# RWKV-7 block on one core: the intra-chunk product of w over 128 rows, and the router's 16 columns streamed eight times

## The chip, the cores and the metric

The kernel runs on one core of one Trainium2 chip. The metric is the device time of one execution in microseconds (us). Three runs of the kernel before took 3162.34, 3146.18 and 3159.18 us, median 3159.18 us.

## What is computed

The reference is one block of a diffusion backbone, over 2048 latent tokens with a prefix of 256 context tokens, width 1024, all in float32. Cut to what bears on the change:

```python
# RWKV-7 time mixing, 8 heads of 64, forward and backward over the tokens
def step(s, inp):
    r_t, w_t, k_t, v_t, a_t, b_t = inp
    sa = einsum('bhvk,bhk->bhv', s, a_t)
    s = s * w_t + sa[..., None] * b_t + v_t[..., None] * k_t
    return s, einsum('bhvk,bhk->bhv', s, r_t)
...
x = x + g1 * (concat([a_x, b_x]) @ w_out)     # time mixing and a short gated convolution
hx = modulate(rmsnorm(x, norm2_g), sh2, sc2)
aff = softmax(hx @ router_w)                  # 16 experts: 16 columns
vals, idx = top_k(swapaxes(aff, 1, 2), 256)   # each expert takes its 256 best tokens
x = x + g2 * scatter_add(silu(xs @ w_gate) * (xs @ w_up) @ w_down * vals)
return rmsnorm(x, final_g)
```

## The kernel before

The program goes through four stages. `proj_phase` (to about 620 us) makes the projections. `wkv_phase` (about 620 to 1860 us) runs the recurrence and fills TensorE's time with other work: the convolution's projections (`conv_gen`, line 262), the convolution's share of the output projection (`conv_out_gen`, line 985), and, from step 20 on, `out_gen`: group norm, output projection, norm and router. `topk` (about 1900 to 1960 us) picks the tokens, and `moe_phase` runs the 16 experts.

The recurrence is cut into chunks of 64 tokens: 4 of context and 32 of latent tokens, so 36 steps s, each for two directions d, forward and backward. For a step and a direction:

- `front` (line 782) multiplies the scaled keys with the scaled queries for all 8 heads and masks the products into `g`, which holds for each head a 128 x 128 block. `solve` (lines 818, 820, on VectorE) and `merge` (lines 839 and 843 on TensorE, copy at line 844 on ScalarE) replace the upper left 64 x 64 part of each block, rows 0 to 63, with the inverse of a triangular matrix.
- `tokmaj` turns the keys to token order (line 798) and allots `uv`, a tile of 128 x 8 x 64 with three buffers: rows 64 to 127 get the values V by a transfer on SyncE's queue (line 803), rows 0 to 63 are written much later with the solved u (line 870).
- `chain` holds the dependent part. `wy` = state times `ar` (line 857: 4 matmuls of 128 rows, 128 columns); then, for each of 8 heads, the intra-chunk part of w is added from rows 64 to 127 of `g` and of `uv` (line 860); ScalarE copies it to `w` (line 863); line 869 applies the inverse, ScalarE copies the result into rows 0 to 63 of `uv` (line 870); line 877 makes the update of the state, VectorE adds it and writes the state `Sb` (lines 883, 886), GpSimd writes the copy `sc` (line 888); line 895 makes the output y.

```python
for h in range(H):
    nc.tensor.matmul(wy[0:64, h], g[64:128, d, hx(h), 0:64], uv[64:128, h], start=False, stop=True, ...)
w = ws[d]
nc.scalar.copy(w[0:64], wy[0:64])
```

The router (`route`, line 1111) is called for each of 16 tiles of 128 tokens: 8 matmuls, each with a 128 x 128 block of the normed tokens as weights and 16 columns of the router's matrix `rt` streamed through. `back` reads the 16 columns of logits from PSUM.

Every float32 matmul is two instructions in the trace; those on the rounded halves ("H" and "L" tiles) are one.

The order of instructions on each engine is not the order of the Python text. The program is traced, and a planner with a simulated time line orders the instructions of each engine by their priority and the time at which it thinks they can start; each engine then runs its own list in order. GpSimd's list in this stage holds part of the scaling of keys and queries (line 766), the copies `sc` (line 888), parts of the convolution and of the second modulation (line 201), and the group norm's gating (lines 1061, 1062). SyncE's list holds the loads and stores, the transfer of V among them. A new `uv` tile can be written only when the tile three before it has been read for the last time, and the planner keeps track of which rows of a tile each instruction touches.

Of the kernel before, what the change touches and what calls it, by code (L numbers as in the profile page):

```python
# [20 lines left out]
KT = 8  # L21
# [9 lines left out]
NE = 16  # L31
# [11 lines left out]
def _dap(t, off, ap):  # L43
    a = t[tuple(slice(None) for _ in t.shape)] if not isinstance(t, bass.AP) else t
    return bass.AP(tensor=a.tensor, offset=a.offset + off, ap=ap)


def two(t, w, j, off=0, n=None):

    lo = NCL // 2 - 1 - j  # L50
    return [_dap(t, c * C * w + off, [[w, C], [1, n or w]]) for c in (lo, lo + 2 * j + 1)]


def two_in(nc, x, rows):

    for q, r in enumerate(rows):
        nc.sync.dma_start(x[64 * q:64 * q + 64], r)
# [636 lines left out]
def wkv_phase(ctx_, tc, k, I, S, fill):  # L694
    nc = tc.nc
    with ExitStack() as ctx:
# [30 lines left out]
        hx = lambda h: h % 2 * HP + h // 2  # L727
        pre = {}

        def tok0(isctx, c):  # L730
            return c * C if isctx else TC + c * C
# [61 lines left out]
        def tokmaj(s, d):  # L793
            isctx, c = order[d][s]
            bk = slots[s, d][2]
            pt = psum.tile([128, HP, 128], F32, name="pbt", tag="pu", bufs=2)
            for p in range(HP):
                nc.tensor.transpose(pt[:, p, :], bk[:, p], k.ident)
            bt = sb.tile([128, HP, 128], F32, name="bt", bufs=2)
            nc.scalar.copy(bt, pt)  # L800
            slots[s, d][2] = bt
            uv = sb.tile([128, H, C], F32, name="uv", bufs=3)
            nc.sync.dma_start(uv[64:128], _dap(S["V"], tok0(isctx, c) * 512, [[512, 64], [64, H], [1, 64]]))
            slots[s, d][3] = uv

# [40 lines left out]
        def chain(s):  # L846
            st_ = []
            if s >= TURN:
                k.y[s] = k.bp.tile([128, H, C], F32, name="oy", tag="ev", bufs=5)
                two_in(nc, k.y[s].rearrange("p h c -> p (h c)"), two(S["Y"], 512, s - TURN))  # L850
            for d in range(2):
                isctx, c = order[d][s]
                ar, g, bt, uv, pc = slots.pop((s, d))
                so = sn = Sb[d]
                wy = psum.tile([128, H, C], F32, name=f"wy{d}")
                for p in range(HP):
                    nc.tensor.matmul(wy[:, 2 * p:2 * p + 2], ar[:, p], so[:, p], start=p == 0, stop=False,
                                     skip_group_check=True)
                for h in range(H):
                    nc.tensor.matmul(wy[0:64, h], g[64:128, d, hx(h), 0:64], uv[64:128, h], start=False, stop=True,  # L860
                                     skip_group_check=True)
                w = ws[d]
                nc.scalar.copy(w[0:64], wy[0:64])
                st_.append((isctx, c, ar, g, bt, uv, pc, so, sn, wy, w))
            for d in range(2):
                isctx, c, ar, g, bt, uv, pc, so, sn, wy, w = st_[d]
                pu = psum.tile([64, H, C], F32, name="pu", bufs=2)
                for h in range(H):
                    nc.tensor.matmul(pu[:, h], g[:, d, hx(h), 0:64], w[:, h], start=True, stop=True)
                nc.scalar.copy(uv[0:64], pu)  # L870
            for d in range(2):
                isctx, c, ar, g, bt, uv, pc, so, sn, wy, w = st_[d]
                if s < NS - 1:
                    sp = psum.tile([128, HP, C], F32, name="ps", tag="pu", bufs=2)
                    for h in range(H):
                        r = slice(64 * (h % 2), 64 * (h % 2) + 64)
                        nc.tensor.matmul(sp[r, h // 2], bt[:, h // 2, r], uv[:, h], start=True, stop=True)
                    f = pc if d == 0 else slots[s + 1, d][4]
                    sc = sb.tile([128, HP, C], F32, name="sc", bufs=4)
                    if s == 0:  # L880
                        nc.vector.tensor_copy(sc, sp)
                    else:
                        nc.vector.tensor_tensor(sc, sp, Sc[d], op=OP.add)
                    for par in range(2):
                        r = slice(64 * par, 64 * par + 64)
                        nc.vector.tensor_tensor(sn[r, :, 64 * par:64 * par + 64], sc[r],
                                                f[r].unsqueeze(2).to_broadcast([64, HP, C]), op=OP.mult)
                    nc.gpsimd.tensor_tensor(sc, sc, f.unsqueeze(2).to_broadcast([128, HP, C]), op=OP.mult)
                    Sc[d] = sc
            for d in range(2):  # L890
                isctx, c, ar, g, bt, uv, pc, so, sn, wy, w = st_[d]
                if isctx:
                    continue
                for h in range(H):
                    nc.tensor.matmul(wy[64:128, h], g[:, d, hx(h), 64:128], uv[:, h], start=False, stop=True,
                                     skip_group_check=True)
                if s < TURN:
                    nc.scalar.copy(uv[64:128], wy[64:128])
                    nc.sync.dma_start(S["Y"][c * C:c * C + C, :], uv[64:128].rearrange("p h t -> p (h t)"))
                else:  # L900
                    half = slice(64 - 64 * d, 128 - 64 * d)
                    nc.vector.tensor_tensor(k.y[s][half], wy[64:128], k.y[s][half], op=OP.add)
# [8 lines left out]
        def ready(s):  # L911
            if s < NS:
                merge(s)
                for d in range(2):
                    tokmaj(s, d)
# [17 lines left out]
        for s in range(NS):  # L933
            chain(s)
            ready(s + 1)
            if s % 2:
                scale((s + 5) // 2)
            begin(s + AHEAD)
            fill(75 // 20 + 1 if s < TURN else 100, s >= TURN)
            if s == TURN:  # L940
                fill(0, True)
# [71 lines left out]
def out_gen(tc, k, I, S):  # L1013

    nc = tc.nc
    bp = k.bp
    wo = load_wo(tc, k, I, S, 0)
    rt = k.cp.tile([128, KT, NE], F32, name="rt")
# [87 lines left out]
        return z  # L1106

    def route(pl, z, n):
        for q in range(4):
            kt = 4 * n + q  # L1110
            nc.tensor.matmul(pl[:, :NE], z[:, q], rt[:, kt], start=kt == 0, stop=kt == KT - 1)

    def spots(j):
        return (slice(0, 64), NCL // 2 - 1 - j), (slice(64, 128), j)
# [10 lines left out]
    def back(j, x, lt=None):  # L1125
        ss = sm("oss", 1)
        square(x, ss)
        r2 = root(ss)
        zs = [flat(j, x, n) for n in range(2)]
        pl = k.bps.tile([128, 512], F32, name="pj")  # L1130
        for n in range(2):
            route(pl, zs[n], n)
        if lt is not None:
            nc.vector.scalar_tensor_tensor(lt, pl[:, :NE], r2, bb, op0=OP.mult, op1=OP.add)
        for half, i in spots(j) if lt is None else ():
            nc.vector.scalar_tensor_tensor(k.lg[half, i % 4, i // 4], pl[half, :NE], r2[half], bb[half], op0=OP.mult,
                                           op1=OP.add)
        if lt is not None:
            return r2
        spill(j, x, r2, "act")  # L1140
# [18 lines left out]
    pl = k.wps.tile([128, 512], F32, name="pl", tag="pu", bufs=2)  # L1159
    for n in halves(LAST, x, y):  # L1160
        square(x[:, 512 * n:512 * n + 512], sums[:, n:n + 1])
        route(pl, flat(LAST, x, n), n)
# [495 lines left out]
```

## Time and profile before

| | |
|---|---|
| median of 3 runs | 3159.18 us (3146.18 to 3162.34) |
| the profiled execution | 3142.96 us |
| its span, first to last instruction | 3141.1 us |
| mean granted TensorE clock over the span | 0.93 |
| TensorE busy (matmuls) | 2881.8 us, 92% |
| VectorE / ScalarE / GpSimd busy | 68% / 44% / 21% |

[...] A row with "x16" merges sixteen instructions in a row, and its time is from the start of the first to the end of the last.

### The profile page before, as it was taken

Reading aid. Unit: us, or ns where it says so; the run is one execution under the profiler, and the core shown is the slowest. Engines: PE = TensorE matmul, PEld = TensorE weight load, DVE = VectorE, ACT = ScalarE, POOL = GpSimd, SP = SyncE. Lnnn points to the kernel's source line nnn. Section 1 sums busy time; section 2 is a strip of 40 time slices with the busy share of each in tenths; the row PEclk is TensorE's granted clock in tenths of the full one; section 3 lists DMA queues with packets and bytes.
Section 4 is the critical chain, followed back from the end, with each engine's and each line's share of the span. In section 5 each row is a group of like instructions: output and inputs, shape, how many; then the busy total and the mean of one; then the engine's idle time right before and its main releaser. Section 6 shows DMA issues by size and latency. Waiting matters only on the chain. (4 is left out here: it accounts for less than half of the span.)

```text
span 3141.1 us, 62585 instructions
## 1 busy us (share of the span) xinstructions
PE 2881.8 (92%) x24367; PEld 2612.9 (83%) x24367; DVE 2141.5 (68%) x4611; ACT 1385.0 (44%) x2279; POOL 667.4 (21%) x893
## 2 busy tenths in 40 slices
PE   6988989889999999999999994999999999999997
PEld 4877978878888888778888873998999899999886
DVE  7688687766666666667767646666666666666776
ACT  6556645423344443224445443444444444444453
POOL 0243242533333322112222121000000000000011
PEclk8989999977999999998788986999999999999998
DMA  6466555666666655766665551666666666666886
GB/s 248 144 201 193 178 175 170 201 170 152 154 169 165 173 141 162 204 176 169 164 151 143 124 165 47 201 219 205 188 204 204 195 197 208 207 203 206 267 285 228
DMA packets 408745, 577.43 MB, mean 184 GB/s; under 512 B 175864, under 2 KB 257912, under 8 KB 407424
## 3 DMA queue, kind: packets, MB, share of 16 engines
q1 hardware_dynamic: 397504, 533.58, 56.4%
q0 software_dynamic: 10656, 38.80, 5.3%
q8 instruction: 191, 3.13, 0.4%
q10 hardware_dynamic: 288, 1.05, 0.1%
q14 instruction: 106, 0.87, 0.1%
HBM read 444.73 MB, written 128.59 MB: 183 GB/s over the span
## 5 line engine op out<-in xcount | busy, mean ns | idle before, releaser
L129 ACT CAST wH<-wr 128x1024 fp32r<-128x1024 f32 (+1 forms) x592 | 528.9, 897 | 844.7 <-PE pg L1429 408.8
L134 DVE TENSOR_TENSOR wL<-wr,wH 128x1024 fp32r<-128x1024 f32 (+1 forms) x586 | 627.6, 1076 | 353.5 <-ACT wH L129 347.6
L1429 PE MATMUL pg<-xH,wH 128*128 128x256 f32 x2048 | 585.4, 286 | 15.8 <-ACT s L1433 15.8
L1429 PE MATMUL pg<-xL,wH 128*128 128x256 f32 x2048 | 576.2, 282 | 0.0
L1429 PE MATMUL pg<-xH,wL 128*128 128x256 f32 x2048 | 575.7, 281 | 0.0
L262 PE MATMUL pj<-hH,wH 128*128 128x256 f32 x1600 | 478.0, 299 | 25.5 <-ACT cu L671 7.4
L262 PE MATMUL pj<-hH,wL 128*128 128x256 f32 x1600 | 469.4, 294 | 23.6 <-DVE wL L134 22.6
L262 PE MATMUL pj<-hL,wH 128*128 128x256 f32 x1600 | 468.1, 293 | 1.4 <-DVE hL L134 1.1
L1429 PEld LDWEIGHTS pg<-xH,wH 128*128 128x128 f32 x2048 | 389.5, 190 | 17.9 <-ACT s L1433 16.5
L1429 PEld LDWEIGHTS pg<-xL,wH 128*128 128x128 f32 x2048 | 389.3, 190 | 1.5
L1429 PEld LDWEIGHTS pg<-xH,wL 128*128 128x128 f32 x2048 | 389.5, 190 | 0.0
L262 PEld LDWEIGHTS pj<-hH,wH 128*128 128x128 f32 x1600 | 318.4, 199 | 37.6 <-DVE cu L674 8.4
L262 PEld LDWEIGHTS pj<-hH,wL 128*128 128x128 f32 x1600 | 316.6, 198 | 30.9 <-DVE wL L134 28.9
L262 PEld LDWEIGHTS pj<-hL,wH 128*128 128x128 f32 x1600 | 318.5, 199 | 5.6 <-DVE hL L134 2.0
L1488 POOL DMA_INDIRECT ACC<-o,it x30 | 50.8, 1694 | 954.4 <-DVE o L1474 800.7
L1446 PE MATMUL pd<-wH,hL 128*128 128x512 f32 x512 | 201.9, 394 | 0.0
L1446 PE MATMUL pd<-wL,hH 128*128 128x512 f32 x512 | 201.9, 394 | 0.0
L1446 PE MATMUL pd<-wH,hH 128*128 128x512 f32 x512 | 199.9, 395 | 0.0
L818 DVE TENSOR_TENSOR x<-X,x 128x120 f32<-128x120 f32 (+12 forms) x540 | 157.8, 296 | 57.7 <-DMA X<-TI 46.0
L820 DVE TENSOR_TENSOR X<-X,x 128x120 f32<-128x120 f32 (+12 forms) x540 | 163.0, 305 | 12.3
L782 PE MATMUL pg<-ar,bk 64*128 64x128 f32 x1152 | 141.0, 323 | 17.1 <-DVE g L784 7.5
L782 PEld LDWEIGHTS pg<-ar,bk 64*128 64x128 f32 x1152 | 114.4, 215 | 33.7 <-issue 13.5
(428 smaller groups left out, 5456.9 us busy)
## 6 DMA issues: line engine op xcount, KB each, us to landing
wr<-in_w_gate_dram SPq DMA_DIRECT2D x128, 512.0 KB, 4.2
wr<-in_w_up_dram SPq DMA_DIRECT2D x128, 512.0 KB, 4.8
wr<-in_w_down_dram SPq DMA_DIRECT2D x128, 512.0 KB, 3.3
wr<-in_w_in_dram SPq DMA_DIRECT2D x208, 256.0 KB, 3.2
bk<-KBD SPq DMA_DIRECT2D x36, 512.0 KB, 5.6
ar<-NR SPq DMA_DIRECT2D x36, 512.0 KB, 5.9
adaw<-in_ada_b_dram SPq DMA_DIRECT2D x32, 512.0 KB, 3.7
inc<-C SPq DMA_DIRECT2D x36, 256.0 KB, 3.1
```

The source lines that it names most:

```text
L129: nc.scalar.copy(H_, src)
L134: (leng or nc.vector).tensor_tensor(L_, src, H_.bitcast(F32), op=OP.subtract)
L262: nc.tensor.matmul(ps, wa[:, kw, :], ha[:, kt, :], start=m == 0, stop=m == 3 * KT - 1)
L782: nc.tensor.matmul(pg[:, p], bk[rows, p], ar[rows, p], start=True, stop=True)
L818: nc.vector.tensor_tensor(tv, X[:, 0:r, t:t + 1].to_broadcast([128, r, m]), x[:, t:t + 1, t + 1:].to_broadcast([128, r, m]), op=OP.mult)
L820: nc.vector.tensor_tensor(X[:, 0:r, t + 1:], X[:, 0:r, t + 1:], tv, op=OP.add)
L1429: nc.tensor.matmul(ps, a[:, ws], b[:, kt], start=i == 0, stop=i == 23)
L1446: nc.tensor.matmul(po[2 * m + n], a[:, f, ms], b[:, ns], start=f == 0 and q == 0, stop=f == FB - 1 and q == 2)
L1488: nc.gpsimd.indirect_dma_start(out=S["ACC"], out_offset=bass.IndirectOffsetOnAxis(ap=ids[m][:, :1], axis=0), in_=o, in_offset=None, comput ...
```

## The change

A memset on GpSimd zeroes rows 0 to 63 of each new `uv` tile. The intra-chunk matmul of w then runs over all 128 rows of `g` and `uv`: the upper 64 rows add products with zeros. The router's 16 columns are read eight times over (a stride of zero), so that each router matmul streams 128 columns and writes 128 columns of PSUM, of which the first 16 are used as before.

```diff
@@ tokmaj
             uv = sb.tile([128, H, C], F32, name="uv", bufs=3)
+            nc.gpsimd.memset(uv[0:64], 0.0)
             nc.sync.dma_start(uv[64:128], _dap(S["V"], tok0(isctx, c) * 512, [[512, 64], [64, H], [1, 64]]))
@@ chain
                 for h in range(H):
-                    nc.tensor.matmul(wy[0:64, h], g[64:128, d, hx(h), 0:64], uv[64:128, h], start=False, stop=True,
+                    nc.tensor.matmul(wy[0:64, h], g[:, d, hx(h), 0:64], uv[:, h], start=False, stop=True,
                                      skip_group_check=True)
@@ route
         for q in range(4):
             kt = 4 * n + q
-            nc.tensor.matmul(pl[:, :NE], z[:, q], rt[:, kt], start=kt == 0, stop=kt == KT - 1)
+            nc.tensor.matmul(pl[:, :128].rearrange("p (a e) -> p a e", e=NE), z[:, q],
+                             rt[:, kt].unsqueeze(1).to_broadcast([128, 128 // NE, NE]), start=kt == 0, stop=kt == KT - 1)
```

## Rows read from the trace of the kernel before

**Rows 1.** The page: busy time of the engines, and granted clock in 40 slices.
```profile
PE 2881.8 (92%) x24367; PEld 2612.9 (83%) x24367; DVE 2141.5 (68%) x4611; ACT 1385.0 (44%) x2279; POOL 667.4 (21%) x893
...
PEclk8989999977999999998788986999999999999998
```

**Rows 2.** Busy time by stretch; after the engines granted clock, DMA share, GB/s.
```profile
620.00:800.00 180.00, 156.73 (x1367) 143.46 (x1367) 118.01 (x279) 58.85 (x97) 64.26 (x96) 0.74 0.68 172
800.00:1440.00 640.00, 602.76 (x6357) 538.13 (x6355) 423.91 (x963) 231.85 (x394) 171.23 (x236) 0.97 0.62 167
1440.00:1895.00 455.00, 435.11 (x4346) 374.94 (x4344) 296.98 (x1014) 212.43 (x420) 108.72 (x158) 0.86 0.61 152
```

**Rows 3.** By stretch, router (L1111) alone: PE, PEld, granted clock, DMA share, GB/s.
```profile
1464.70:1495.20 30.50, 1.86 (x16) 1.86 (x16) 1.00 0.49 127
1495.40:1512.30 16.90, 0.00 (x0) 0.00 (x0) 0.50 0.80 210
...
1529.60:1536.20 6.60, 0.33 (x2) 0.22 (x2) 0.50 0.66 161
...
1539.90:1543.00 3.10, 0.00 (x0) 0.00 (x0) 0.50 0.47 157
...
1563.80:1570.30 6.50, 0.39 (x2) 0.29 (x2) 0.50 0.64 155
...
1594.50:1611.20 16.70, 0.00 (x0) 0.00 (x0) 0.50 0.37 89
...
1632.00:1635.10 3.10, 0.00 (x0) 0.00 (x0) 0.50 1.19 193
...
1656.00:1669.00 13.00, 3.59 (x16) 3.48 (x16) 0.50 0.60 132
...
1697.00:1703.00 6.00, 3.60 (x16) 3.49 (x16) 0.50 0.98 175
...
1816.30:1819.40 3.10, 0.00 (x0) 0.00 (x0) 0.50 0.02 5
...
1878.00:1880.90 2.90, 0.00 (x0) 0.00 (x0) 0.50 0.99 353
```

**Rows 4.** The same for the intra-chunk matmuls of w (L860) alone.
```profile
741.10:778.40 37.30, 3.93 (x32) 3.56 (x32) 0.50 0.64 158
1444.20:1464.50 20.30, 3.93 (x32) 3.55 (x32) 0.50 0.79 209
```

**Rows 5.** The time line of TensorE just before the fall at 1495.3 us.
```profile
1492.96 1.86 PE L1111 MATMUL pj<-rt,oxt 128*128 128x16 f32 x16
```

**Rows 6.** The time line, 1440 to 1480 us: runs of weight loads, one per matmul.
```profile
1441.41 1.64 PEld L1027 LDWEIGHTS pj<-rb,ones 128*128 128x128 f32 x14
...
1446.63 1.77 PEld L860 LDWEIGHTS wy<-uv,g 64*64 64x64 f32 x16 [0.22 <-issue]
...
1457.61 1.78 PEld L869 LDWEIGHTS pu<-w,g 128*64 128x64 f32 x16 [0.22 <-issue]
...
1468.03 0.97 PEld L857 LDWEIGHTS wy<-Sb,ar 128*128 128x128 f32 x8
...
1477.44 0.54 PEld L860 LDWEIGHTS wy<-uv,g 64*64 64x64 f32 x8
```

**Rows 7.** GpSimd's memset of line 716: count, shortest, median, longest in ns.
```profile
L716 POOL MEMSET w<- x2: 520/521/522, 618.9 to 619.3; 64x512 f32 x2
```

**Rows 8.** The time line at 1758 us: V is asked for, and w starts.
```profile
1758.40 0.45 SPq L803 DMA_DIRECT2D uv<-V  x1
...
1762.98 1.14 PE L860 MATMUL wy<-uv,g 64*64 64x64 f32 x16 [1.99 <-DMA uv<-V]
```

**Rows 9.** The time line at 1526 us: w starts ahead of merge's last copy.
```profile
1526.29 1.14 PE L860 MATMUL wy<-uv,g 64*64 64x64 f32 x16
...
1538.22 0.57 ACT L844 COPY g<-pm 32x512 f32<-32x512 f32 x1 [1.14 <-PE pm L843]
```

**Rows 10.** GpSimd's waits, 630 to 1900 us: total us, times, longest.
```profile
POOL sc L888 <- DVE Sb L886: 262.2, 64, 24.0
```

## The prediction

> **What bounds the kernel now.** I read the page first: TensorE is busy 92% of the span, no other engine passes 68%, and the granted clock, slice by slice, is below 0.9 in few places [rows 1]. [...] I then cut the span by stage [rows 2]. The recurrence has two weak stretches: 620 to 800 us, with a mean clock of 0.74, and 1440 to 1895 us, with 0.86. Between them, with the convolution's 256-column matmuls as filler, it is 0.97. [...]
>
> The third view asks what TensorE did before each fall. In 1440 to 1895 us I count 15 stretches at 0.50. Nine of them follow straight on the router's matmuls [rows 3]. The first: 16 of them end at 1494.8 us [rows 5], and the clock is 0.50 from 1495.3 to 1512.4 us. The same happens at 1529, 1564, 1594 and 1632 us, and four more times from 1816 to 1881 us, of which the first and the last are shown. These nine are 16.9 + 6.6 + 6.5 + 16.7 + 3.1 us, and 15.4 us for the last four: 65.2 us. A tenth, 3.1 us at 1540 us, follows on 16 matmuls of line 860, the intra-chunk part of w. Inside three more low stretches the two edited kinds stand too: 32 of line 860 in 741 to 778 us and 32 in 1444 to 1464 us [rows 4], 16 router matmuls in each of 1656 to 1669 and 1697 to 1703 us [rows 3]; four stretches, 37.3 + 20.3 + 13.0 + 6.0 = 76.6 us.
>
> What the edited kinds share is that TensorE is occupied by them and does little: the router streams 16 columns for every 128 x 128 load of weights, line 860 uses half the rows. The change fills the empty columns and rows.
>
> **Router.** 128 matmuls, 256 instructions. Fourteen instructions of the same form, 128 rows with 16 columns (line 1027), take 1.64 us at the full clock, 0.117 each; eight with 128 columns (line 857) take 0.97, 0.121 each [rows 6]. The weight load sets the distance in both. So widening costs 0.004 us each by these rows, 256 x 0.004 = 1.0 us, and I take 1. The bounds are 0 and, if the streaming did not hide, the whole of a 128-column instruction again, 31 us.
>
> **w over 128 rows.** Sixteen of line 860 take 1.77 us at the low clock, sixteen of line 869, which already are 128 rows by 64 columns, 1.78 [rows 6]. 1152 instructions at nothing each: 0 us, bounds 0 and 1152 x 0.001 = 1 us.
>
> **The memset.** 72 of them, the size of line 716: 0.521 us each [rows 7], 37.5 us more on GpSimd, which is busy 109 of 455 us in the late stretch [rows 2]. It needs the same buffer to come free as the transfer of V, and w waits for both. The shortest of the 72 distances from the issue of V to w's first matmul is 4.6 us [rows 8], with w waiting for V at its end. The memset fits nine times. I take 0, with ends of 0 and 37.5 us: the cover is the transfer of V and, after it, GpSimd's idle time. What it can run into is GpSimd's own list: behind the memset stand the scaling of keys and queries and `sc`, ahead of it may stand an instruction that waits.
>
> **The added dependence on merge.** w now reads rows 0 to 63 of `g`, so it waits for merge's copy (line 844). In 28 of 36 steps that copy ends before w begins. In eight it doesn't, the shown one by 12.5 us [rows 9]; in the first step w ran 78 us ahead for nothing. In these w moves behind the copy, but line 869 has to wait for the copy anyway, so what is added to the chain is w itself and its copy: 16 x 0.068 = 1.1 us [rows 6] and about 0.6 us like the copy shown, 1.7 us, 7 times: 12 us of the recurrence. TensorE has other work queued (it idles 20 of 455 us), so I take 3 us, with ends of 0 and 12. Next in line behind w's copy is line 869, which is late by as much.
>
> **The clock.** [...] Of the 76.6 us in the four other stretches the fall itself stays, as other narrow work stands before it, and I let the clock come back halfway through: 38 us, a gain of 19. Sum 53 us, with ends of 0 and (68.3 + 76.6) / 2 = 72. Not all of it arrives: work that runs faster meets waits (in rows 2 VectorE is busy 297 of 455 us), and new falls can appear where there was none, since every instruction moves. I keep eight tenths: 42 us.
>
> Sum: 42 - 1 - 0 - 3 = 38 us off. Against the profiled execution, 3142.96 us, that is 3105 us. That execution was 16.2 us faster than the median of the three runs; from the median, 3159.18, it is 3121 us, which I forecast.
>
> **Rival: no difference.** The clock may follow only the time for which TensorE is occupied, not how much of it. Then filling columns and rows, at the same distance from matmul to matmul, changes nothing, and the time is the median plus the costs, 3159 + 4 = 3163 us. Against it: in 1440 to 1895 us TensorE is occupied 96% of the time, more than the 94% of the stretch before, and has the lower clock [rows 2]. [...] A second road to the same result: the planner gets other costs (128 columns instead of 16, a memset, a new dependence), reorders the stage, and as many falls come up elsewhere. Chance of both together 0.20.
>
> **Rival: slower.** The memset sits on GpSimd's list behind the `sc` of the step before, which waits for the state (64 waits, 262 us, the longest 24 us [rows 10]). The state is also what line 857 starts from, and from there to w lie only its 0.97 us. Where the memset starts after `sc`, it can end after line 857 and w waits; each such wait idles TensorE, and in the stretch where it idles most (157 of 180 us busy) the clock is lowest [rows 2], so the gain goes too. It decides as soon as the memset ends over 0.97 us after the state. The price is at most the memset for each of 72 tiles, 37.5 us: 3159 + 37 = 3197 us. Against it: the buffer comes free 4.6 us or more before w, mostly while `sc` of the step before is not yet due, and a planner that places by readiness puts the memset early. Chance 0.10.
>
> **Numbers.** The forecast, with its gain anywhere from 16 to 75 us, has 0.70. A difference of 0.5%, 16 us, is about what a measurement of this kernel can tell from none (the three runs span 16 us). The low end is the whole of the clock's 72 us and a little for falls that I did not count: 3082 us. The high end takes in the no-difference rival with all of the merge's 12 us, 3171 us; it leaves out most of the slower rival. Of the forecast's 0.70 some 0.02 falls short of 16 us, and of the no-difference rival some 0.04 still gains over 16: faster 0.72, same 0.18, slower 0.10.
>
> **What would show it.** In the profile after: the granted clock in the stretch from step 21 to the top-k at 0.93 or more, and no fall straight behind the router; the router's 16 instructions still within 1.9 us, line 860's sixteen within 1.1 us at the full clock; line 860 now shown as 128 rows; 72 memsets of about 0.52 us and no long wait of line 860 for them; TensorE's total busy time down by some 40 us, nearly all between 1440 and 1895 us, and the stages before 620 us and after the top-k as long as they were. The prediction is wrong if the router's widened matmuls are still followed by falls, if the number of low stretches stays at about fifteen, if waits for GpSimd stand among TensorE's largest, or if the time saved lies in a stage that the edits don't touch.

## The result, and the profile after

The change takes 3106.82 us (median of 4 runs, 3096.77 to 3115.09), the kernel before beside it 3152.68 us: a ratio of 0.9866, 95% interval 0.9828 to 0.9904, so 1.3%, or some 42 us by the ratio and 46 us by the medians. The forecast was a gain of 38 us.

The profiled execution after took 3115.09 us (span 3113.2 us, granted clock 0.945). The page, and busy time by stretch with the columns of [rows 2]; PE is TensorE's matmuls, PEld its weight loads, and the granted clock is a share of full speed:

```profile
PE 2823.5 (91%) x24367; PEld 2567.4 (82%) x24367; DVE 2151.2 (69%) x4611; ACT 1379.1 (44%) x2275; POOL 701.1 (23%) x965
...
PEclk8989999979999999999999996999999999999998
```
```profile
620.00:800.00 180.00, 146.08 (x1436) 134.66 (x1434) 123.53 (x291) 62.83 (x104) 73.53 (x113) 0.85 0.68 178
800.00:1440.00 640.00, 596.89 (x6270) 535.25 (x6266) 424.32 (x942) 229.62 (x389) 187.59 (x268) 0.96 0.61 166
1440.00:1895.00 455.00, 399.25 (x4457) 345.68 (x4456) 329.08 (x1158) 220.10 (x457) 130.84 (x199) 0.93 0.62 156
```

TensorE runs the same 24367 matmuls and is busy 58 us less; the span of this execution is only 28 us shorter, so TensorE also idles 30 us more. The stretch from 1440 to 1895 us has a clock of 0.93 instead of 0.86 [rows 2], although it now also holds the beginning of the top-k, where TensorE is nearly idle.

Where the time went is read from the starts of two kinds of matmul. Lines of one source line each: count, shortest, median, longest ns, first and last start. First the top-k's first matmul before, then the router and the same top-k matmul after:

```profile
L1258 PE MATMUL pa<-ident,lg x16: 311/311/365, 1900.2 to 1901.5; 64*64 64x64 f32 x16
```
```profile
L1113 PE MATMUL pj<-rt,oxt x240: 275/275/582, 1498.4 to 1862.4; 128*128 128x128 f32 x120
...
L1261 PE MATMUL pa<-ident,lg x16: 311/311/365, 1868.6 to 1869.9; 64*64 64x64 f32 x16
```

From the first router call to the top-k it was 1900.2 - 1493.0 = 407.2 us [rows 5] and is 370.2 us: 37 us less. From there to the end it is 1240.9 and 1244.6 us, and the projections ahead took about 9 us longer in this execution; neither is touched by the change. From the recurrence's first matmul (line 782) to the first router call it is 862.9 and 859.5 us, 3 us less; that stretch returns further down.

The same stage after, with the columns of [rows 3] and of the router alone; the stretches are cut where the clock changes:

```profile
1474.80:1478.00 3.20, 0.00 (x0) 0.00 (x0) 0.50 1.03 228
1478.20:1505.30 27.10, 2.05 (x16) 1.86 (x16) 1.00 0.54 161
...
1529.40:1536.00 6.60, 3.78 (x16) 3.49 (x16) 0.50 0.87 198
...
1573.90:1676.00 102.10, 5.95 (x48) 5.60 (x48) 1.00 0.66 163
...
1751.30:1853.50 102.20, 10.75 (x80) 9.54 (x80) 1.00 0.54 150
1853.70:1856.90 3.20, 0.00 (x0) 0.00 (x0) 0.50 1.01 394
```

Nine falls are left where there were fifteen, and they hold some 37 us instead of 123. None comes straight behind the router. One stretch of 102 us holds 48 router instructions at full clock, another 80. What stands before a fall now is, for example, this, on the time line just ahead of the fall at 1474.7 us:

```profile
1469.23 1.15 PE L861 MATMUL wy<-uv,g 128*64 128x64 f32 x16
1472.80 1.12 PE L861 MATMUL wy<-uv,g 128*64 128x64 f32 x16 [2.42 <-DMA uv<-V]
1473.84 0.81 PE L840 MATMUL pm<-tz,g 32*32 32x32 f32 x20
```

The widened w stands there with a wait for V, in which TensorE idled 2.42 us. A pause of this kind stands ahead of all nine. The rows below take the 4 us ahead of a fall, with the columns of [rows 2]: the figure behind the comma is how long TensorE was busy in them. First come two of the falls behind the router before the change, then three of the nine after it, namely the one shown, the one with the most idle time and the one with the least:

```profile
1491.30:1495.30 4.00, 4.00 (x60) 3.75 (x57) 3.91 (x20) 1.16 (x2) 0.71 (x1) 1.00 0.64 148
1590.30:1594.30 4.00, 4.00 (x41) 3.72 (x42) 3.88 (x25) 1.46 (x4) 0.00 (x0) 1.00 0.50 114
```
```profile
1470.70:1474.70 4.00, 1.90 (x37) 1.82 (x38) 2.36 (x15) 0.87 (x2) 1.74 (x2) 1.00 0.68 187
1501.40:1505.40 4.00, 0.07 (x2) 0.10 (x2) 4.00 (x9) 3.41 (x10) 2.48 (x3) 1.00 0.82 280
1535.50:1539.50 4.00, 3.12 (x67) 2.65 (x66) 3.61 (x15) 1.16 (x2) 0.00 (x0) 0.92 1.08 203
```

Before the change, ahead of nine of the fifteen falls, TensorE had idled less than 0.3 of those 4 us. These nine held some 85 of the 123 us, and eight of them had matmuls of 16 columns within the 4 us. Ahead of the other six it had idled 1.2 to 3.4 us. After the change it had idled 0.9 to 3.9 us ahead of every one of the nine. So there were two kinds of falls, those without a pause and those behind a pause, and only the second kind is left. Which part of the change does what is the question of the experiments.

### The profile page after: what moved, and what is told of

Same layout as the page of the kernel before. It is cut to its first block, busy times and chain, and to the rows that moved or that the text cites. A ratio compares the mean times of both kernels' runs of the same rounds, so it can differ in the third digit from the quotient of the medians.

```text
span 3113.2 us, 62779 instructions
## 1 busy us (share of the span) xinstructions
PE 2823.5 (91%) x24367; PEld 2567.4 (82%) x24367; DVE 2151.2 (69%) x4611; ACT 1379.1 (44%) x2275; POOL 701.1 (23%) x965
## 5 line engine op out<-in xcount | busy, mean ns | idle before, releaser
L819 DVE TENSOR_TENSOR x<-X,x 128x120 f32<-128x120 f32 (+9 forms) x540 | 163.0, 305 | 65.7 <-DMA X<-TI 53.3
L821 DVE TENSOR_TENSOR X<-X,x 128x120 f32<-128x120 f32 (+9 forms) x540 | 168.1, 314 | 12.0
L782 PE MATMUL pg<-ar,bk 64*128 64x128 f32 x1152 | 125.0, 312 | 31.8 <-POOL em L749 8.1
L782 PEld LDWEIGHTS pg<-ar,bk 64*128 64x128 f32 x1152 | 103.8, 208 | 47.5 <-POOL ar L766 11.5
```

What stands on the lines that cost most here:

```text
L782: nc.tensor.matmul(pg[:, p], bk[rows, p], ar[rows, p], start=True, stop=True)
L819: nc.vector.tensor_tensor(tv, X[:, 0:r, t:t + 1].to_broadcast([128, r, m]), x[:, t:t + 1, t + 1:].to_broadcast([128, r, m]), op=OP.mult)
L821: nc.vector.tensor_tensor(X[:, 0:r, t + 1:], X[:, 0:r, t + 1:], tv, op=OP.add)
```

## The experiments

Theory: the clock follows how much of the array TensorE fills while it is occupied, and both parts of the change fill it. Rivals: the gain is only another order of instructions; or it is one part's alone; or the memset costs time. Every run lists its mean granted clock c, and the low-clock time below (the time at a granted clock of 0.50) is 2 (1 - c) x span, averaged over a kernel's executions. That takes the clock to be either 1.00 or 0.50: of 10470 pieces of 0.3 us in the profiled execution before, 8966 are at 1.00, 1406 at 0.50 and 98 between them. As an estimate, half of the low-clock time is what a higher clock can save: sixteen of the router take 1.86 us at 1.00 and 3.48 us at 0.50 [rows 3]. The low-clock time is that of the whole program; of the 440 us before, some 125 lie in the router's stage. Each ratio is to the runs of the kernel before that were taken beside that kernel (their medians lie between 3145.53 and 3152.68 us), so two kernels are better compared by their ratios than by their medians.

| kernel | median us | ratio to before (95%) | mean clock | low-clock us |
|---|---|---|---|---|
| before (the 29 runs beside the router alone) | 3147.95 | | 0.930 | 440 |
| whole change, first | 3106.82 | 0.9866 (0.9828 to 0.9904) | 0.947 | 328 |
| whole change, again | 3100.66 | 0.9867 (0.9844 to 0.9890) | 0.948 | 324 |
| router at 128 alone | 3101.55 | 0.9842 (0.9815 to 0.9868) | 0.944 | 349 |
| w over 128 rows, with the memset | 3136.15 | 0.9973 (0.9950 to 0.9996) | 0.938 | 391 |
| memset alone | 3139.47 | 0.9961 (0.9940 to 0.9982) | 0.931 | 434 |
| router at 32 | 3139.40 | 0.9978 (0.9950 to 1.0005) | 0.936 | 403 |
| router at 64 | 3110.69 | 0.9889 (0.9866 to 0.9912) | 0.940 | 373 |
| router at 256 | 3145.26 | 1.0000 (0.9978 to 1.0021) | 0.942 | 363 |
| router and its bias at 128 | 3108.23 | 0.9878 (0.9852 to 0.9904) | 0.944 | 350 |
| memset, w's first head over 128 rows | 3149.30 | 1.0006 (0.9980 to 1.0031) | 0.933 | 421 |
| whole, merge in its own tile | 3119.73 | 0.9912 (0.9877 to 0.9947) | 0.946 | 339 |
| router at 128, merge in its own tile | 3102.04 | 0.9853 (0.9816 to 0.9890) | 0.948 | 322 |
| whole, four uv buffers | 3126.65 | 0.9927 (0.9900 to 0.9954) | 0.945 | 343 |

### One part at a time

**The router alone.** Line 860 as before, and no memset.

> Only the router is widened to 128 columns; w keeps 64 rows and there is no memset. Theory (the clock follows how much of the array TensorE fills while it is occupied): the nine low stretches behind the router, 65 us, go, the fall behind w stays; gain 65 / 2 x 0.8 = 26 us, so about 3127 us against a median before of 3153; low-clock time in the stage from the first router call to the top-k from 123 us down to about 60. Rival 1 (the gain is only another order of instructions): falls still come straight behind the router, and the gain can be anything, as large in the kernel with 32 columns. Rival 2 (the gain comes from w alone): 3153 us, within 8.

3101.55 us: the whole gain, 46 us by the medians, where 26 were expected. The low-clock time falls by 440 - 349 = 91 us, and half of that is 45 us. Nothing else is needed to explain it.

**w alone.**

```diff
+            nc.gpsimd.memset(uv[0:64], 0.0)
-  nc.tensor.matmul(wy[0:64, h], g[64:128, d, hx(h), 0:64], uv[64:128, h], ...)
+  nc.tensor.matmul(wy[0:64, h], g[:, d, hx(h), 0:64], uv[:, h], ...)
```

> Only w is widened to 128 rows, with the memset; the router keeps 16 columns. Theory: falls still come behind the router in most of the nine places, the low stretches in which w stands end sooner; gain 8 to 20 us, about 3140 us. The two parts together give about what the whole change gave (46 us) or a little less than their sum. Rival 1: no relation between what is widened and where falls vanish. Rival 3 (the memset costs time on GpSimd): slower than before by up to 37 us.

**The memset alone.**

> Only the memset of rows 0 to 63 is added; w keeps 64 rows and the router 16 columns. The planner's order changes as much as with w widened. Theory: no clock gain, the memsets hidden: 3153 us, between 3 faster and 8 slower; falls behind the router as before. Rival 1 (order): a gain like that of w widened, 8 to 20 us or more. Rival 3: slower by 10 to 37 us, with TensorE waiting for GpSimd.

3136 and 3139 us: the same within their intervals. The memset costs nothing; it is even 0.4% faster than before with no more clock to show for it, so moving the instructions about is worth up to some ten microseconds. Widening w on top of it moves the time by 3 us by the medians (by the ratios w is even the slower of the two), although 434 - 391 = 43 us of low clock go, half of which would be 21 us. The sum of the parts' gains, 46 + 12 us, is more than the 46 us of the whole.

### The router by columns

```diff
-            nc.tensor.matmul(pl[:, :NE], z[:, q], rt[:, kt], ...)
+            nc.tensor.matmul(pl[:, :N].rearrange("p (a e) -> p a e", e=NE), z[:, q],
+                             rt[:, kt].unsqueeze(1).to_broadcast([128, N // NE, NE]), ...)
```

N = 32, 64 and 256, nothing else changed.

> The router is widened to 32 columns instead of 128; nothing else. TensorE's time per router matmul is the same, the order of instructions differs from before by about as many places as with 128 columns. Theory: a small part of the gain, 0 to 12 us (about 3147 us), and most of the falls behind the router stay. Rival 1 (order): the same gain as with 128 columns.

> Router at 64 columns, nothing else. Theory (the clock follows how much of the array is filled): with 32 columns 7 us came off, with 128 columns 46; 64 columns lie between, 20 to 45 us off, and falls straight behind the router are rarer than with 16 (10 falls) but not gone. Rival (order): no relation to the number of columns.

> Router at 256 columns. No fall behind the router, as with 128. But here the streaming no longer hides behind the weight load: 256 columns of float32 in 2 instructions should hold TensorE for about 0.22 us each instead of 0.112, 256 x 0.1 = 27 us more. Theory: 15 to 25 us off instead of 46. Rival (streaming stays hidden, or the clock gains more with more columns): 46 us off or more.

Off the medians of before come 9, 35, 46 and 1 us for 32, 64, 128 and 256 columns; the low-clock time is 403, 373, 349 and 363 us. With 32 columns the order of TensorE's instructions in the trace differs from before in about as many places as with 128, so another order as such is not the reason. The falls behind the router are still there; this is 32 columns, router alone:

```profile
1541.00:1545.10 4.10, 1.97 (x16) 1.86 (x16) 1.00 0.88 260
1545.30:1555.30 10.00, 0.00 (x0) 0.00 (x0) 0.50 0.50 88
1578.70:1582.60 3.90, 1.97 (x16) 1.86 (x16) 1.00 0.52 118
1582.80:1592.80 10.00, 0.00 (x0) 0.00 (x0) 0.50 0.56 148
```

Sixteen weight loads of the router take 1.86 us with 32 columns, as with 128. The first router call on the time line with 128 columns, and with 256:

```profile
1495.12 1.86 PEld L1112 LDWEIGHTS pj<-rt,oxt 128*128 128x128 f32 x16
```
```profile
1498.25 3.33 PEld L1112 LDWEIGHTS pj<-rt,oxt 128*128 128x128 f32 x16
```

With 256 columns they take 3.33 us, 0.208 each instead of 0.116 (0.22 instead of 0.112 was expected): 1.47 us more for each of 16 tiles, 23.5 us. That takes most of the clock's gain of (437 - 363) / 2 = 37 us; the rest up to the measured 0 to 1 us, some 13 us, I did not trace. A gain of 15 to 25 us was expected here. Of the widths with such a row, 128 columns are the most at which sixteen still take 1.86 us.

**The bias matmuls too.** Line 1027, 16 instructions with 16 columns, stands before a fall in the router-alone kernel (that line alone, by stretch):

```profile
1443.00:1446.00 3.00, 1.74 (x14) 1.64 (x14) 1.00 1.00 309
1446.30:1466.60 20.30, 0.00 (x0) 0.00 (x0) 0.50 0.77 205
```

> Router at 128 columns, w as before, and the router's bias matmuls (line 1027, 16 instructions of the same 16-column form, which stand before the fall at about 1444 us) at 128 columns too. Theory: the low stretch of 20 us behind them goes in most executions; a further 0 to 10 us beyond the router alone, about 3095 us against a before of 3148. Rival (that fall has another cause): as the router alone, 3101 us.

A miss: 3108.23 us, not better than the router alone. The fall at 1446 us is gone in its trace, but the low-clock time over its executions is the same, 350 us. What falls in its place is not shown.

### What w gives and takes

**The whole again, beside the others.**

> The whole change again, beside the router alone. Theory now: w over 128 rows gives no clock that the router doesn't give, so 3100 to 3107 us, ratio 0.984 to 0.987. Rival: w gives its own 10 to 19 us on top of the router's, about 3090 us. Second rival: the 72 memsets on GpSimd's list take something back, 3105 to 3115 us.

3100.66 us: w adds nothing to the router. Yet the low-clock time is 324 us, 25 less than with the router alone, which should be worth 12 us. Something takes them back. Where they go can be read from one execution of each kernel, with the columns of [rows 2], from the recurrence's first matmul to the first router call: before, the router alone, the memset alone, w with the memset, the whole change.

```profile
630.10:1493.00 862.90, 809.62 (x8276) 725.76 (x8276) 576.07 (x1342) 314.25 (x535) 241.67 (x333) 0.91 0.63 166
628.60:1495.20 866.60, 814.24 (x8274) 730.55 (x8275) 576.40 (x1342) 314.51 (x535) 242.39 (x333) 0.91 0.62 166
632.10:1500.70 868.60, 810.85 (x8343) 727.82 (x8343) 582.18 (x1366) 316.58 (x538) 267.30 (x381) 0.92 0.63 167
631.40:1488.50 857.10, 785.33 (x8343) 707.68 (x8343) 588.92 (x1362) 315.91 (x539) 269.94 (x381) 0.94 0.63 169
638.90:1498.40 859.50, 786.51 (x8343) 708.50 (x8343) 587.52 (x1360) 315.39 (x539) 267.74 (x381) 0.94 0.63 168
```

From the first router call to the top-k, the memset alone, then w with the memset:

```profile
1500.70:1895.60 394.90, 371.96 (x3712) 322.66 (x3711) 256.55 (x897) 180.06 (x367) 103.24 (x164) 0.86 0.61 150
1488.50:1881.80 393.30, 358.65 (x3712) 310.96 (x3711) 263.48 (x901) 182.85 (x369) 103.81 (x165) 0.90 0.61 151
```

With w over 128 rows TensorE's work gets 25.5 us shorter in the first stretch than with the memset alone (785.33 against 810.85 us), but the stretch only 11.5 us; TensorE idles 72 us there instead of 58. In the second stretch it is 13 us less work and 2 us less time. The whole change against the router alone gives the same picture in the first stretch: 28 us less work, 7 us less time. So in these executions most of what TensorE gains by the clock with w over 128 rows turns into idle time. Why it idles is the next question. The two new waits of w, on merge and on the memset, are the suspects; in the trace of the whole change TensorE waits at w itself 1.1 us in all for merge's copy, and no wait of it for the memset shows, so they could act only through what stands behind them.

**The waits without the rows.** Only the first of eight heads takes 128 rows.

```diff
+                    rows = slice(0 if h == 0 else 64, 128)
-  nc.tensor.matmul(wy[0:64, h], g[:, d, hx(h), 0:64], uv[:, h], ...)
+  nc.tensor.matmul(wy[0:64, h], g[rows, d, hx(h), 0:64], uv[rows, h], ...)
```

> The memset, and w over 128 rows for the first of eight heads only; router at 16 columns. Every wait of the widened w is there, an eighth of the filled rows. Theory A: the costs without the gain: time less half of the low-clock time 2935 to 2945 us (2923 with the memset alone, 2943 with all heads wide), low-clock time near that of the memset alone (434 us), so 3150 to 3160 us, slower than the memset alone (3139). Rival B, part one (the wait for merge costs nothing, wide matmuls cost by themselves): as the memset alone, 3136 to 3143 us.

3149.30 us, 10 us more than the memset alone and 13 more than with all heads wide; by the ratios 14 and 10 us, and the intervals of 1.0006 and 0.9973 overlap. This points to two effects and does not prove them. Filling the rows of the seven other heads takes 421 - 391 = 30 us of low clock away, half of it 15 us, and 10 to 13 us come off. The new dependence of w, or the order that the planner makes of it, would cost the 10 to 14 us, with a little less low clock.

**Merge's wait taken away.** Merge writes into a tile of its own, zeroed once, which line 869 uses; `sc` gives up a buffer for the room.

```diff
+        gm = st.tile([128, 16, 64], F32, name="gm0")
-            nc.scalar.copy(g[lo, :, hi], pm2[lo])
+            nc.scalar.copy(gm[lo, :, hi], pm2[lo])
-  nc.tensor.matmul(pu[:, h], g[:, d, hx(h), 0:64], w[:, h], ...)
+  nc.tensor.matmul(pu[:, h], gm[:, 8 * d + hx(h)], w[:, h], ...)
```

> The whole change, but merge writes its result into a tile of its own (one buffer, lower rows zero), which line 869 uses, so w no longer waits for merge; sc has three buffers instead of four for the room. Theory A (over all runs, w over 128 rows takes about 45 us of low clock away, worth 22 us, and gives 15 to 20 us back because w now waits for merge): the time apart from the clock, that is the time less half of the low-clock time, falls from 2939 to 2942 us in the whole change to about 2927, and the time to 3085 to 3095 us, faster than the whole change and than the router alone (3102). Rival B (what is given back is the wait for the memset, or another order of instructions): no better than 3100 us.

> Control for the kernel with merge's own tile: router at 128 columns, w over 64 rows, no memset, merge into its own tile, sc with three buffers. Theory A: as the router alone, 3102 us within 8. If it is faster than that by as much as the kernel with w widened, the gain is the tile's and not w's; if slower, the tile itself costs.

Theory A, that the wait for merge eats w's gain, falls: 3119.73 us with w wide, 3102.04 us with w over 64 rows and no memset. Without the wait for merge, w and its memset cost 18 us here, and there is not even less low clock (339 against 322 us). The 322 us also weaken what was read from the whole change: this kernel, with w over 64 rows, has as little low clock as the whole (324 us). Another order of instructions can move the low-clock time by as much as w's rows.

**The memset's wait.** TensorE's waits for GpSimd, 630 to 1860 us (total us, times, longest), in the whole change:

```profile
PE pbt L798 <- POOL bk L766: 8.2, 2, 6.3
PE pg L782 <- POOL em L749: 8.1, 3, 6.2
PE pg L782 <- POOL ar L766: 5.9, 4, 2.2
```

The same three kinds are 2.6 us before. GpSimd's longest waits for its memset, 630 to 1870 us:

```profile
POOL uv L803 <- PE wy L896: 65.2, 17, 13.8
...
POOL uv L803 <- DMA Y<-uv: 50.8, 23, 4.4
```

The memset stands waiting for its buffer. The theory (C) is that the scaling of keys and queries behind it comes late for this.

```diff
-            uv = sb.tile([128, H, C], F32, name="uv", bufs=3)
+            uv = sb.tile([128, H, C], F32, name="uv", bufs=4)
```

> The whole change with four buffers for uv instead of three: a new tile comes free about half a step earlier, so the memset no longer stands waiting at the head of GpSimd's list (126 us in 42 waits in the whole change) and the scaling of keys and queries behind it is not held up (TensorE waited 22 us for GpSimd). Theory C (that wait eats what w's fuller rows give): TensorE's waits for GpSimd under 6 us, time less half of the low clock about 2928 us, and 3085 to 3095 us, faster than the router alone (3102). Rival D (w's fuller rows are worth nothing in time, and what differs beside is the planner's order): 3098 to 3110 us again, even if the waits for GpSimd go.

```profile
PE pbt L798 <- POOL bk L766: 10.3, 2, 6.7
PE pg L782 <- POOL em L749: 10.0, 1, 10.0
PE pg L782 <- POOL ar L766: 6.5, 5, 2.0
```

3126.65 us, slower than the whole change, and the waits did not go: GpSimd still waits 102 us for the memset's buffer, after 126 us with three buffers. The edit did not do what it was for, so it tests nothing; that the planner moved the memset along with its buffer is a guess. Against theory C stands the kernel with the memset alone: TensorE's waits of these three kinds are 19 us there, and it is not slower than before. Which wait takes the 10 to 18 us, or whether it is the order, stays open.

## Why the prediction was right

- **What bounds the stage** held for the router: TensorE's clock. Half of the low clock that went is the time that went, 45 of 46 us with 128 columns and 32 against 35 us with 64. It did not hold for w, as below. TensorE was busy 435 of the 455 us [rows 2], and 11.5 of the other 20 stand in the 4 us ahead of six of the fifteen falls; ahead of the other nine it had idled less than 0.3 us. And "straight on" was said too easily: at 1632, 1816 and 1837 us other matmuls stood between the router and the fall, ahead of the falls at 1857 and 1878 us TensorE had been idle too, and at 1540 us merge's small blocks stood among w's matmuls. Two slips: the "three more low stretches" are four, as the sum has them, and the low end of 3082 us is a gain of 77 us, not of 75.
- **The router's cost** held: sixteen still take 1.86 us, and the widening costs nothing that can be seen up to 128 columns. That the weight load sets the distance was my reading of [rows 6]: at a clock of 1.00 line 1027, with 16 columns behind loads of 128 x 128, has 0.117 us from one to the next, line 857, with 128 columns behind such loads, 0.121, and line 860, with 64 columns behind loads of 64 x 64, 0.54 / 8 = 0.068. **The clock's gain by the router** was mis-sized. I gave it the nine stretches behind it and half of the two in which it stood, (65.2 + 9.5) / 2 x 0.8 = 30 us; it measured 46. 91 us of low clock went instead of the 75, and all of it arrived, not eight tenths. In the sum of 53 us, 34 stand for the ten falls, half of their 68.3 us; no run shows these 34 us, and what the runs showed in their place is the 46 us of the router alone.
- **The clock's gain by w** is the step that failed. From the tenth fall and half of the two stretches of [rows 4] I took (3.1 + 28.8) / 2 x 0.8 = 13 us into the sum. Beside the memset alone it measured 3 us, on top of the router nothing. The low clock that goes was not too high, 43 us against the 32 that I assumed; what failed is that eight tenths of its half arrive. TensorE's work got shorter, and TensorE idled for most of the difference. The two sizes were off in opposite ways, and that the sum of 38 came out near 46 is in part luck.
- **The memset at 0** held: 72 of them, 0.518 us, and alone not slower than before. But one sign that I gave for a wrong prediction did come: waits for GpSimd are among TensorE's largest, in the three kinds shown up from 3 to 22 us, on the scaling of keys and queries and what belongs to it, which stand behind the memset in GpSimd's list. I had named that list and priced it at nothing. As the memset alone has these waits too and is not slower, they are not shown to cost time.
- **w's waits at 3 us, with an end of 12**: one head wide costs 10 us more than the memset alone by the medians and 14 by the ratios, at the end of that range or past it, not the value that I took; and I put it on merge, which the kernel with merge's own tile does not bear out.
- **The rival of no difference**, that the clock follows occupied time alone, fell: with 16, 32 and 128 columns sixteen of the router take 1.86 us, and the low-clock time goes 440, 403, 349 us (373 with 64 columns). Idle time stands ahead of falls as well in these traces: ahead of the nine falls that are left TensorE had idled 0.9 to 3.9 of 4 us.
- **The slower rival** did not come in the form that I gave it: what GpSimd's memset waits for longest is its buffer, and no wait of w for the memset shows in the trace of the whole change.
- Of the signs, the falls behind the router are gone, sixteen of w take 1.01 us, and the saved time lies between the first router call and the top-k. The number of falls went to nine, not to the few that stand alone in my list: new ones came, as allowed for, and all nine stand behind idle time.

No version beat the change clearly: the router's edit alone does the same in one statement, without memset and with w as it was.

## What to carry to other kernels

Where TensorE is occupied nearly all the time and its clock still falls, look at what stands just before each fall, and tell falls behind a pause from falls without one. Here sixteen float32 matmuls with 16 columns behind weight loads of 128 x 128 took 1.86 us, as long as with 128 columns, and streaming the same columns again, up to 128, took away the falls behind the router and 91 us of low clock at no cost; with 256 columns sixteen took 3.33 us, and 1 us came off instead of 46. Check, too, that a higher clock arrives as time: in the kernels with w over 128 rows it turned mostly into idle time (25.5 us less work and 11.5 us less time than with the memset alone, up to the first router call), and the padding's new operand, a zeroed half, came with new waits of TensorE for GpSimd (22 us in the three kinds shown instead of 2.6). And test the parts of a change alone: here one of two gave the whole gain.

## What the runs showed of the hardware

Between 1440 and 1895 us of the profiled execution before, TensorE's clock fell from 1.00 to 0.50 fifteen times: nine times after it had idled less than 0.3 of the last 4 us, eight of these with matmuls of 16 columns behind weight loads of 128 x 128 in those 4 us, and six times after it had idled 1.2 to 3.4 of them. After the change it fell nine times, each time after 0.9 to 3.9 us of idling in the last 4 us, and never straight behind the router's matmuls of 128 columns. With 32 columns, the router alone, it was 0.50 from 1545.3 and from 1582.8 us, with sixteen of the router in the 4 us ahead.

With all eight heads of w over 128 rows, half of them zeros, the low-clock time is 391 us, with one head 421. That rows of zeros do this is not shown, as another order of instructions can do as much (322 us with the router widened and merge in its own tile, 349 without that tile, w over 64 rows in both).

Sixteen matmuls of the router take 1.86 us with 16, 32 and 128 columns at a clock of 1.00, and 3.33 us with 256.
